# The first 1024 tokens' value projection, block by block, with TensorE run in beforehand

## The chip, the cores and the metric

The kernel runs on one core of a Trainium2 chip. What counts is the device time of one execution in microseconds (us). A core has TensorE (PE in the profile; its weight loads are PEld), VectorE (DVE), ScalarE (ACT), GpSimd (POOL) and SyncE (SP, which here issues the DMAs). PSUM, where TensorE writes its sums, has 8 banks of 128 x 512 words of 32 bits.

## The reference

A trunk of two layers over 1024 tokens of width 1024, all in float32. Layer 0 mixes tokens by dilated attention, layer 1 by gated linear attention; each mixer is followed by a squared-ReLU MLP. The change touches the very start: the first norm and the value part of the first projection.

```python
def rmsnorm(x, w):
    y = xf * lax.rsqrt(jnp.mean(xf * xf, axis=-1, keepdims=True) + NORM_EPS)
    return (y * w.astype(jnp.float32)).astype(x.dtype)

def dilated_attention(h, w_in, w_out):
    qkv = (h @ w_in).reshape(B, S, N_GROUPS, 3, ATTN_HEADS, HEAD_DIM)   # 3 groups
    ...
        v = qkv[:, :, g, 2].astype(jnp.float32)
    ...

h = rmsnorm(x, norm_mix_w[0]);  x = x + dilated_attention(h, ...)
```

So for each of three column groups g a 1024 x 1024 matrix of weights is applied to the normed tokens to give the values.

## The kernel before

A product in float32 is made of three in a rounded format: each operand is a rounded part ("hi", written by ScalarE: `dh` for weights, `a12h` for tokens) and a remainder ("lo", written by VectorE: `dl`, `a12l`), and hi x hi, hi x lo and lo x hi are summed in one bank.

The value projection uses Strassen's scheme (Winograd's form): tokens and columns are halved, and seven products of half matrices take the place of eight. The token operands are `a11`, `a12` (first 512 tokens, first and second half of the width), `a21`, `a22` (last 512 tokens) and sums of them, `s1` to `s4`; `s1` is `a21 + a22`. They are made once and serve all three groups. Work goes in *steps*, numbered n = 14 g + 2 q + m: group g, product q (0 to 6), half m of the depth. A step has 24 products of 128 x 512: 4 blocks of 128 tokens, 2 slices of depth, 3 combinations. Steps 0 and 1 multiply `a12` into the four banks `pB`, steps 2 and 3 `a11` into four banks `pA`; steps 4 and 5 (`s1`) follow in `pB`, 6 and 7 (`s2`) in `pA`, 8 and 9 (`s4`) in `pB`. Steps 14 and 15 are steps 0 and 1 of group 1: the same `a12`, other weights.

The class `Values` has a method for each part of a step: `load` (512 KB of weights, a DMA from SP), `total` (VectorE's sum of weight blocks, where the scheme has one), `rounded` (`dh`, L808), `remain` (`dl`, L814), `product` (the matmuls, L829), `sums` (`copy`, ScalarE takes a bank out, L839; `add`, VectorE adds the other bank, L844, and SP stores the result `c`). The first product's banks are copied out as `c11` when its step is done, and the second's are added. `prep` is `rounded` and `remain`.

The class `Halves` makes the token operands, in pairs of blocks (256 tokens): `norm` (ScalarE squares and sums a row, L243; VectorE and ScalarE make the root; VectorE scales, giving `xn`, L252), `turn` (TensorE transposes 128 x 128 pieces of `xn` with `ident` into a bank `pT`, L334; ScalarE copies it out into `a`, L336), `cut` (ScalarE rounds `a`, L344, VectorE takes the remainder, L346).

There is no scheduler: each engine's instructions stand in the order in which the code issues them, and each engine works its list in order, waiting where an operand or a buffer is not ready. Buffers come from pools: `h8` (12 of 8 KB for each partition), `k4` (25 of 4 KB, for weights in all forms and `xn`), `t2` (8 of 2 KB), and the 8 banks. The order at the start is written out by hand, and from step 8 on is a loop:

```python
for n in range(8, vals.STEPS):
    ...
    vals.sums(n)
    vals.prep(n + 2)
    vals.load(n + 5)
    vals.product(n)
```

At the start, steps 0 to 3 are done for blocks 0 and 1 as soon as these two blocks are turned and cut, then for blocks 2 and 3, and then step 4 follows; blocks 4 to 7 are normed and turned in between, since `s1` needs them.

Of the kernel before, what the change touches and what calls it, by code (L numbers as in the profile page):

```python
# [19 lines left out]
P = 128  # L20
D = 1024
S = 1024
NB = S // P
# [6 lines left out]
EPS = 1e-5  # L30
# [11 lines left out]
def hybrid_trunk(ctx, tc, x, norm_mix, norm_mlp, norm_fin, a_in, a_out, g_in, g_up, g_b, g_nw,  # L42
                 g_out, m_up, m_down, tab, msk, gmask, ident_d, out):
    nc = tc.nc
    pe, act, dve, pool, sp = nc.tensor, nc.scalar, nc.vector, nc.gpsimd, nc.sync
# [454 lines left out]
    class Up:  # L500
# [244 lines left out]
    class Values:  # L745

        STEPS = 14 * NG
        small = False
        BLOCKS = ((1, 0), (0, 0), (0, 1), (1, 1), (1, 1), None, (1, 0))

        def __init__(self):
# [7 lines left out]
        def load(self, n):  # L759
# [3 lines left out]
            if q == 5:  # L763
                return
            k, c = self.BLOCKS[q]
            if q in (1, 2):
# [63 lines left out]
                                  stop=m == 1 and k == 1 and v == 2, skip_group_check=True)  # L830

        def copy(self, name, s, t, g):
            if name == "c22":
                if t % 2 == 0:
                    self.pair = k4([P, 2, 512], F32, "c22")
# [15 lines left out]
        def sums(self, n):  # L851

            g, q, m = self.place(n)
            if q == 0 and g and m == 0:
                for t in range(4):
                    self.add("c21", "B", t, g - 1)
            for t in (2 * m, 2 * m + 1):
                if q == 1:
                    self.copy("c11", "B", t, g)
# [18 lines left out]
    class Mixed(Values):  # L878

        STEPS = 28  # L880
        small = True

        def __init__(self):
            super().__init__()
# [80 lines left out]
    scale = HD ** -0.5  # L965
# [299 lines left out]
            at(t + 10, lambda half=half: join(half), 9)  # L1265


    x0 = []
    vals = Values()
    for p in range(NB // 2):  # L1270
        t = h8([P, 2, D], F32, "x0")
        for i in range(2):
            sp.dma_start(t[:, i, :], x[0, 256 * p + 128 * i:256 * p + 128 * i + 128, :])
        x0.append(t)
        if p == 0:
            wbc = load_norm_w(norm_mix[0])
            sp.dma_start(ident, ident_d)
            for n in range(4):
                vals.load(n)
# [5 lines left out]
    vals.remain(0)  # L1285
    hs.cut("a12", 0)
    hs.turn(0, (0, 1))
    vals.prep(1)
    hs.cut("a11", 0)
    vals.prep(2)  # L1290
    vals.prep(3)
    hs.norm(1)
    for n in range(3):
        vals.product(n, [0, 1])
    hs.norm(2)
    hs.turn(1)
    vals.product(3, [0, 1])
    hs.cut("a12", 1)
    hs.cut("a11", 1)
    vals.load(4)  # L1300
    vals.load(5)
    hs.turn(2)
    hs.sum1(0)
    vals.total(4)
    hs.rstd(3)
    hs.norm(3)
    for n in range(2):
        vals.product(n, [2, 3])
    hs.cut("s1", 0)
    vals.rounded(4)  # L1310
    hs.turn(3)
    vals.remain(4)
    vals.product(2, [2, 3])
    vals.total(5)
    vals.sums(2)
    hs.sum1(1)
    hs.cut("s1", 1)
    vals.sums(3)
    vals.rounded(5)
    vals.product(3, [2, 3])  # L1320
    vals.remain(5)
    vals.load(6)
    vals.load(7)
# [3 lines left out]
    hs.cut("s2", 0)  # L1327
    vals.rounded(6)
    hs.cut("s2", 1)
    vals.sums(4)  # L1330
    vals.sums(5)
    vals.remain(6)
    vals.load(8)
    vals.product(4)
# [2 lines left out]
    vals.product(5)  # L1337
    for c in range(2):
        hs.cut("s4", c)
    hs.sum3()  # L1340
    vals.load(9)
    for n in range(6, 8):
        vals.sums(n)
        vals.load(n + 4)
        vals.product(n)
        vals.prep(n + 2)
        if n == 6:
            for c in range(2):
                hs.cut("s3", c)
        else:  # L1350
            for c in range(2):
                hs.cut("a22", c)
    vals.load(12)
    for n in range(8, vals.STEPS):
        if n == 12:
            ctab = h8([P, 2, S], F32, "tab")
            sp.dma_start(ctab[:, 0, :], tab[:, 0, :])
            sp.dma_start(ctab[0:64, 1, :], tab[64:128, 1, :])
            sp.dma_start(ctab[64:128, 1, :], tab[0:64, 1, :])
        if n == vals.STEPS - 2:  # L1360
            heads = Heads(vals.h)
# [7 lines left out]
        vals.prep(n + 2)  # L1369
        vals.load(n + 5)  # L1370
        vals.product(n)
    for t in range(4):
        vals.add("c21", "B", t, NG - 1)
# [630 lines left out]
    for half in range(2):  # L2004
        ps = bank("pd")
# [7 lines left out]
        l = lrT[:, 512 * half:512 * half + 512]  # L2013
# [62 lines left out]
```

## Time and profile before

| | |
|---|---|
| median of 3 runs | 2612.7 us (2612.32 to 2613.21) |
| the profiled execution | 2613.06 us, span 2611.3 us |
| mean granted TensorE clock | 0.999 |
| first instruction of TensorE | 8.89 us |
| first product of the value projection | 12.96 us |
| first product of step 4 | 44.58 us |

The span goes from the first to the last instruction; times of single instructions are counted from its start. A row of the timeline gives start, length, engine, line, operation, what it writes and reads, how many follow each other, and in brackets for how long the engine stood idle before and for whom it waited. Matmuls are pipelined: a row's length (0.39 us) is longer than the distance to the next start.

### The profile page before, as it was taken

What the parts mean: (1) busy time and instruction counts of PE and PEld (TensorE: products, weight loads), DVE (VectorE), ACT (ScalarE), POOL (GpSimd) and SP (SyncE); (2) the same over time, 40 slices, a digit from 0 to 9 for tenths busy, and PEclk for the clock granted to TensorE, in tenths of its full rate; (3) what the DMA queues carried; (4) which work ended last, traced back from release to release, by engine and by line L of the source; (5) the groups of instructions that cost most, each with busy time, mean ns of one, the idle gap of its engine ahead of it and who ended that gap; (6) DMA issues with size and microseconds to landing.
All of it is one profiled execution on the core that took longest, in us unless ns stands there. A gap on an engine that the chain in (4) does not pass through costs nothing.

```text
span 2611.3 us, 33042 instructions
## 1 busy us (share of the span) xinstructions
PE 2586.3 (99%) x12144; PEld 2157.3 (83%) x12144; DVE 1858.9 (71%) x2986; ACT 1276.7 (49%) x2319; POOL 1.8 (0%) x7
## 2 busy tenths in 40 slices
PE   8999999999999999999999999999999999999998
PEld 6888888888888888888888887878888888888887
DVE  7645888888888768666657577977658866666566
ACT  6332455555556446555533345654326545553343
POOL 0000000000000000000000000000000000000000
PEclk9999999999999999999999999999999999999999
DMA  5533465655556733454775452463513544396543
GB/s 190 169 129 124 103 161 131 163 147 150 155 151 183 227 121 128 167 169 137 283 252 185 137 194 93 133 199 97 187 66 123 170 153 157 131 355 200 189 146 125
DMA packets 327010, 423.12 MB, mean 162 GB/s; under 512 B 19808, under 2 KB 192224, under 8 KB 326848
## 3 DMA queue, kind: packets, MB, share of 16 engines
q1 hardware_dynamic: 326848, 421.01, 51.0%
q8 instruction: 95, 1.56, 0.3%
q14 instruction: 67, 0.55, 0.1%
HBM read 279.71 MB, written 116.06 MB: 152 GB/s over the span
## 4 chain that ended last, share of the span: by engine, by line
PE 87%; DVE 8%; ACT 3%; issue 1%; DMA 1%; SPq 0%; ACTq 0%; DVEq 0%
PE pX L598 16%; PE pB L1581 13%; PE pV L598 11%; PE pA L1581 10%; PE pY L598 5%; PE pZ L598 5%; PE pB L829 5%; PE pd L215 3%; PE pd L213 3%; PE pd L214 3%; PE pA L829 3%; PE pO L1017 2%; PE pS L976 2%; PE pP L1003 1%; DVE dl L814 1%
## 5 line engine op out<-in xcount | busy, mean ns | idle before, releaser
L1581 PE MATMUL pB<-dh 128*128 128x512 f32 x512 | 199.4, 389 | 0.0
L1581 PE MATMUL pB<-dh,dl 128*128 128x512 f32 x512 | 199.2, 389 | 0.0
L1581 PE MATMUL pB<-dl,dh 128*128 128x512 f32 x512 | 199.2, 389 | 0.0
L222 DVE TENSOR_TENSOR dl<-sin,dh 128x1024 fp32r<-128x1024 f32 x112 | 136.5, 1218 | 44.6 <-ACT dh L219 44.2
L219 ACT ACTIVATE dh<-sin 128x1024 fp32r<-128x1024 f32 x112 | 117.8, 1052 | 89.7 <-PE pB L1581 32.5
L219 ACT ACTIVATE dh<-kept 128x1024 fp32r<-128x1024 f32 x64 | 67.9, 1061 | 183.4 <-DVE kept L1546 137.8
L598 PE MATMUL pV<-s4h,wd 128*128 128x512 f32 x448 | 150.8, 398 | 0.0
L1581 PE MATMUL pA<-dh,dl 128*128 128x512 f32 x384 | 149.4, 389 | 0.0
L1581 PE MATMUL pA<-dl,dh 128*128 128x512 f32 x384 | 149.4, 389 | 0.0
L1581 PE MATMUL pA<-dh 128*128 128x512 f32 x384 | 149.4, 389 | 0.0
L992 ACT ACTIVATE pt<-pt,orow 128x128 f32<-128x128 f32 (+1 forms) x192 | 84.8, 443 | 96.7 <-DVE orow L990 94.6
L1581 PEld LDWEIGHTS pB<-dh,dl 128*128 128x128 f32 x512 | 96.1, 188 | 20.1
L1581 PEld LDWEIGHTS pB<-dh 128*128 128x128 f32 x512 | 96.1, 188 | 19.9
L1581 PEld LDWEIGHTS pB<-dl,dh 128*128 128x128 f32 x512 | 96.1, 188 | 19.8
L536 DVE TENSOR_TENSOR wal<-raw,wah 128x512 fp32r<-128x512 f32 x112 | 76.2, 686 | 42.9 <-ACT wah L535 42.9
L607 ACT ACTIVATE c<-c 128x512 f32<-128x512 f32 x64 | 40.4, 632 | 122.6 <-DVE c L635 78.9
L598 PEld LDWEIGHTS pV<-s4h,wd 128*128 128x128 f32 x448 | 84.2, 188 | 17.7 <-DVE rb L623 0.2
L222 DVE TENSOR_TENSOR dl<-kept,dh 128x1024 fp32r<-128x1024 f32 x64 | 78.3, 1224 | 25.1 <-ACT dh L219 19.3
L536 DVE TENSOR_TENSOR wbl<-t,wbh 128x1024 fp32r<-128x1024 f32 x56 | 68.6, 1225 | 38.3 <-ACT wbh L535 38.3
L990 DVE CUSTOM_DVE_ANT_0 pt<-pS,masks 128x128 f32<-128x128 f32 (+1 forms) x192 | 58.2, 347 | 51.2 <-PE pS L976 51.2
L598 PE MATMUL pY<-a12h,wah 128*128 128x512 f32 x224 | 89.5, 400 | 0.0
L598 PE MATMUL pZ<-a22h,wgh 128*128 128x512 f32 x224 | 89.3, 399 | 0.0
(336 smaller groups left out, 7364.2 us busy)
## 6 DMA issues: line engine op xcount, KB each, us to landing
sin<-acts SPq DMA_DIRECT2D x112, 512.0 KB, 3.8
raw<-in_mlp_w_up_dram SPq DMA_DIRECT2D x64, 512.0 KB, 6.0
acts<-s SPq DMA_DIRECT2D x64, 512.0 KB, 3.4
raw<-in_mlp_w_down_dram SPq DMA_DIRECT2D x64, 512.0 KB, 4.7
raw<-in_attn_w_in_dram SPq DMA_DIRECT2D x96, 256.0 KB, 4.6
cw<-c SPq DMA_DIRECT2D x192, 128.0 KB, 2.3
acts<-c SPq DMA_DIRECT2D x64, 256.0 KB, 2.1
kept<-in_mlp_w_down_dram SPq DMA_DIRECT2D x32, 512.0 KB, 5.8
```

The costliest lines, as they stand in the source:

```text
L213: pe.matmul(ps, sh, mh, start=start, stop=False)
L214: pe.matmul(ps, sh, ml, start=False, stop=False)
L215: pe.matmul(ps, sl, mh, start=False, stop=stop)
L219: act.activation(hi, src, AF.Copy)
L222: dve.tensor_tensor(lo, src, hi.bitcast(F32), op=OP.subtract)
L536: self.remain(lambda: dve.tensor_tensor(lo, src, hi.bitcast(F32), op=OP.subtract))
L598: pe.matmul(st[b], u[:, k, :], v, start=first and k + n == 0, stop=k == 3 and n == 2, skip_group_check=True)
L829: pe.matmul(self.acc[s][t], a[:, c], b[:, k, :], start=fresh and m + k + v == 0, stop=m == 1 and k == 1 and v == 2, skip_group_check=True)
L976: pe.matmul(ps[:, i, :128 * n], self.qT[:, 128 * b:128 * b + 128], self.kT[:, k0:k0 + 128 * n], start=True, stop=True)
L990: dve.tensor_tensor_reduce(pt[:, i, :128 * n], ps[:, i, :128 * n], masks[:, m0:m0 + 128 * n], -scale, 1e38, op0=OP.add, op1=OP.min, accum_ ...
L992: act.activation(pt[:, i, :128 * n], pt[:, i, :128 * n], AF.Exp, scale=-1.0, bias=m, accum_out=self.row[:, r, HD:HD + 1])
L1581: pe.matmul(self.acc[s][t], a[:, k, c], b[:, k, :], start=fresh and m + k + v == 0, stop=m == 7 and k == 1 and v == 2, skip_group_check=True)
```

## The change

It rewrites the order of the start and has these parts.

- Run-in: POOL clears a tile `warm`, and TensorE does 26 matmuls of 128 x 512 in bf16 on it, before anything else.
- Loads: the first block's rows and the norm weight `wbc` come in halves; the order on SP becomes first block, half of `wbc`, `ident`, weights of step 0, other half of `wbc`, weights of step 1, block 1, weights of steps 2 and 3, blocks 2 to 5, weights of steps 14 and 15, blocks 6 and 7.
- Blocks 0 to 3 are handled singly: `sq` and `lne` make the root's start on ScalarE, `nvz` one Newton step on VectorE, `xn` half a block, `tr` four transposes into one bank. `hi` and `lo` round and take the remainder straight from that bank; `ac` copies it into `a` later (the sums need it).
- Products: steps 0 to 3 are done for block 0 first, then block 1, 2 and 3; after blocks 4 and 5 are turned, steps 14 and 15 on block 0, then blocks 6 and 7 are turned, then steps 14 and 15 on blocks 1 to 3, then step 4.
- The `c11` of group 1 is copied out then, into two buffers of `k4`, and kept until the add of step 18. The later loop leaves out steps 14 and 15 (`plan`); the adds of group 0's last product (`c21`) move from step 14 to step 16.
- `sums(2)` to `sums(5)` stand earlier (`cp`, `ad`); after step 6, `cut("s3")` and `sum3` stand one later.

```diff
-    x0 = []
+    x0 = [h8([P, 2, D], F32, "x0") for _ in range(NB // 2)]
...
+    warm = t2([P, 512], BF16, "warm")
+    pool.memset(warm, 0.0)
+    dve.memset(eps, EPS)
+    ps = bank("warm")
+    for _ in range(26):
+        pe.matmul(ps, warm[:, 0:P], warm, start=True, stop=True)
+    for c in (0, 512):
+        sp.dma_start(x0[0][:, 0, c:c + 512], x[0, 0:128, c:c + 512])
...
+    load_wbc(512)
+    sp.dma_start(ident, ident_d)
+    vals.load(0)
+    load_wbc(0)
+    vals.load(1)
+    load_rows(1)
+    vals.load(2)
+    vals.load(3)
+    load_rows(2, 3, 4, 5)
+    vals.load(14)
+    vals.load(15)
+    load_rows(6, 7)
...
+    def sq(b):
+        r = root0[b] = sm([P, 8], "root")
+        junk = t2([P, D], BF16, "junk")
+        act.activation(junk, rows0(b), AF.Square, accum_out=r[:, 0:1])
+    def lne(b):
+        r = root0[b]
+        act.activation(r[:, 2:3], r[:, 0:1], AF.Ln, scale=1.0 / D, bias=eps)
+        act.activation(r[:, 3:4], r[:, 2:3], AF.Exp, scale=-0.5)
+    def nvz(b):
+        ss, nv, t, y, z = (root0[b][:, i:i + 1] for i in range(5))
+        dve.tensor_scalar(nv, ss, -0.5 / D, -0.5 * EPS, op0=OP.mult, op1=OP.add)
+        dve.scalar_tensor_tensor(z, y, nv, y, op0=OP.mult, op1=OP.mult)
+        dve.scalar_tensor_tensor(z, z, 1.5, y, op0=OP.add, op1=OP.mult)
...
+    def hi(b, half):
+        ps, h, l, a = spot(b, half)
+        act.activation(h, ps, AF.Copy)
+    def lo(b, half):
+        ps, h, l, a = spot(b, half)
+        dve.tensor_tensor(l, ps, h.bitcast(F32), op=OP.subtract)
+    def ac(b, half):
+        ps, h, l, a = spot(b, half)
+        act.activation(a, ps, AF.Copy)
...
-    hs.norm(0, (512, 768, 0, 256), 256)
-    vals.rounded(0)
-    hs.turn(0, (2, 3))
...
-    for n in range(3):
-        vals.product(n, [0, 1])
-    hs.norm(2)
-    hs.turn(1)
-    vals.product(3, [0, 1])
...
+    hi(0, 1)
+    lo(0, 1)
+    xn(0, 0)
+    rh(1)
+    pr(0, 0)
+    sq(1)
+    rl(1)
+    tr(0, 0)
+    lne(1)
+    hi(0, 0)
+    rh(2)
+    nvz(1)
+    xn(1, 1)
+    pr(1, 0)
...
+    rh(15)
+    pr(1, 3)
+    ad(1)
+    rl(15)
+    hs.xn[2] = [xn0.pop(4), xn0.pop(5)]
+    pr(2, 3)
+    hs.turn(2)
+    sq(7)
...
+    pr(14, 0)
+    hs.xn[3] = [xn0.pop(6), xn0.pop(7)]
+    pr(15, 0)
+    hs.turn(3)
+    hs.cut("s1", 0)
     vals.load(4)
     vals.load(5)
...
-    for n in range(8, vals.STEPS):
+    plan = [n for n in range(8, vals.STEPS) if n // 14 not in vals.ahead or n % 14 > 1]
...
+        if n % 14 == 2 and n // 14 in vals.ahead:
+            for t in range(4):
+                vals.add("c21", "B", t, n // 14 - 1)
```

(`rh`, `rl`, `pr` are `rounded`, `remain` and `product` on the named blocks; `cp`, `ad` are `copy` and `add` of `c11`.)

How the order stands, first on TensorE at its beginning. The numbers behind the names tell one tile from another: `pB_213` and `pB_214` are the banks of blocks 0 and 1, `dh_142`/`dl_158` the weights of step 0. Before, behind sixteen transposes:

```order
L334 MATMUL pT_170<-ident_68,xn_133 128x128
L829 MATMUL pB_213<-dh_142,a12h_160 128x512
L829 MATMUL pB_213<-dl_158,a12h_160 128x512
L829 MATMUL pB_213<-dh_142,a12l_161 128x512
L829 MATMUL pB_214<-dh_142,a12h_160 128x512
L829 MATMUL pB_214<-dl_158,a12h_160 128x512
L829 MATMUL pB_214<-dh_142,a12l_161 128x512
```

Now, behind the run-in (`pB_187` is block 0's bank, `dh_173` of step 0, `dh_185` of step 1, `dh_210` of step 2; `xn_171` is block 0, `xn_215` block 1):

```order
L1342 MATMUL pT_175<-ident_68,xn_171 128x128 x4
L830 MATMUL pB_187<-dh_173,a12h_154 128x512
L830 MATMUL pB_187<-dl_180,a12h_154 128x512
L830 MATMUL pB_187<-dh_173,a12l_155 128x512
...
L1342 MATMUL pT_202<-ident_68,xn_171 128x128 x4
L830 MATMUL pB_187<-dh_185,a12h_154 128x512
...
L1342 MATMUL pT_226<-ident_68,xn_215 128x128 x4
L830 MATMUL pA_235<-dh_210,a11h_156 128x512
```

Six products of one block now stand behind four transposes, and step 1 behind four more.

VectorE at the same place, before:

```order
L252 SCALAR_TENSOR_TENSOR xn_133<-x0_93,y_123,wbc_96 128x256
L814 TENSOR_TENSOR dl_158<-raw_99,dh_142 128x1024
L346 TENSOR_TENSOR a12l_161<-a_145,a12h_160 128x4x256
L814 TENSOR_TENSOR dl_178<-raw_101,dh_176 128x1024
L346 TENSOR_TENSOR a11l_181<-a_144,a11h_180 128x4x256
L814 TENSOR_TENSOR dl_186<-kept_103,dh_184 128x1024
```

and now:

```order
L815 TENSOR_TENSOR dl_200<-raw_136,dh_185 128x1024
L1328 TENSOR_SCALAR root_197<-root_197 128x1
L1329 SCALAR_TENSOR_TENSOR root_197<-root_197 128x1
L1330 SCALAR_TENSOR_TENSOR root_197<-root_197 128x1
L1336 SCALAR_TENSOR_TENSOR xn_215<-x0_93,root_197,wbc_130 128x512
L1354 TENSOR_TENSOR a11l_157<-pT_202,a11h_156 128x4x128
L815 TENSOR_TENSOR dl_224<-kept_139,dh_210 128x1024
L1336 SCALAR_TENSOR_TENSOR xn_215<-x0_93,root_197,wbc_130 128x512
L815 TENSOR_TENSOR dl_245<-kept_141,dh_232 128x1024
L1354 TENSOR_TENSOR a12l_155<-pT_226,a12h_154 128x4x128
```

Block 1's root and `xn` now stand between the weights' remainders of steps 1, 2 and 3, and remainders of tokens are taken from a bank.

TensorE once more, where the last blocks are turned. Before, the transposes of blocks 6 and 7 (`xn_370`, `xn_371`) stood between steps 1 and 2 of blocks 2 and 3:

```order
L829 MATMUL pB_216<-dh_176,a12l_161 128x512
L334 MATMUL pT_408<-ident_68,xn_370 128x128
L334 MATMUL pT_408<-ident_68,xn_371 128x128
...
L334 MATMUL pT_426<-ident_68,xn_371 128x128
L829 MATMUL pA_243<-dh_184,a11h_180 128x512
```

Now step 3 of block 3 (`pA_238`) and steps 14 and 15 of block 0 (`dh_410`, `dh_418`) stand ahead of them (`xn_407`), behind the last bank of blocks 4 and 5 (`xn_396`):

```order
L334 MATMUL pT_456<-ident_68,xn_396 128x128
L830 MATMUL pA_238<-dh_232,a11h_156 128x512
L830 MATMUL pA_238<-dl_245,a11h_156 128x512
...
L830 MATMUL pB_489<-dh_410,a12h_154 128x512
L830 MATMUL pB_489<-dl_412,a12h_154 128x512
...
L830 MATMUL pB_489<-dh_418,a12h_154 128x512
...
L334 MATMUL pT_505<-ident_68,xn_407 128x128
```

Products of group 1 thus stand between the turns of blocks 4, 5 and of blocks 6, 7.

More of the change, by code (lines that the diff above doesn't have):

```diff
@@ L748, in hybrid_trunk @@
         small = False
+        ahead = (1,)
         BLOCKS = ((1, 0), (0, 0), (0, 1), (1, 1), (1, 1), None, (1, 0))
@@ L832, in copy @@
         def copy(self, name, s, t, g):
-            if name == "c22":
+            if name == "c22" or (name == "c11" and g in self.ahead):
                 if t % 2 == 0:
-                    self.pair = k4([P, 2, 512], F32, "c22")
+                    self.pair = k4([P, 2, 512], F32, name)
                 c = self.pair[:, t % 2, :]
@@ L858, in sums @@
                 if q == 1:
-                    self.copy("c11", "B", t, g)
+                    if g not in self.ahead:
+                        self.copy("c11", "B", t, g)
                 elif q == 2:
@@ L881, in hybrid_trunk @@
         small = True
+        ahead = ()
         def __init__(self):
@@ L1265, in plan_merges @@
             at(t + 10, lambda half=half: join(half), 9)
-    x0 = []
+    x0 = [h8([P, 2, D], F32, "x0") for _ in range(NB // 2)]
     vals = Values()
[L1270 to L1279, printed above, removed]
+    eps = sm([P, 1], "eps")
@@ new lines, in rows0, with load_rows @@
+    def rows0(b):
+        return x0[b // 2][:, b % 2, :]
+    def load_rows(*bs):
+        for b in bs:
+            sp.dma_start(rows0(b), x[0, 128 * b:128 * b + 128, :])
+    warm = t2([P, 512], BF16, "warm")
[6 more added lines that the diff above has]
+        sp.dma_start(x0[0][:, 0, c:c + 512], x[0, 0:128, c:c + 512])
+    wbc, row = k4([P, D], F32, "wbc"), norm_mix[0]
@@ L1280, in hybrid_trunk, with load_wbc @@
+    def load_wbc(c):
+        sp.dma_start(wbc[:, c:c + 512], bass.AP(tensor=row.tensor, offset=row.offset + c, ap=[[0, P], [1, 512]]))
+    load_wbc(512)
[10 more added lines that the diff above has]
+    load_rows(6, 7)
     sp.dma_start(masks, msk)
     hs = Halves(x0, wbc, vals, None)
-    hs.norm(0, (512, 768, 0, 256), 256)
-    vals.rounded(0)
@@ L1284, in hybrid_trunk @@
-    hs.turn(0, (2, 3))
[L1285 to L1292, printed above, removed]
-    for n in range(3):
-        vals.product(n, [0, 1])
-    hs.norm(2)
-    hs.turn(1)
-    vals.product(3, [0, 1])
-    hs.cut("a12", 1)
-    hs.cut("a11", 1)
+    for name in ("a12", "a11"):
+        vals.h[name] = Split(hs.one(name + "h", F32R), hs.one(name + "l", F32R))
+    for half in range(2):
+        hs.a[0, half] = hs.one("a", F32)
@@ new lines, in xn, with tr, spot @@
+    def xn(b, half):
+        if b not in xn0:
+            xn0[b] = k4([P, D], F32, "xn")
+        sl = slice(512 * half, 512 * half + 512)
+        dve.scalar_tensor_tensor(xn0[b][:, sl], rows0(b)[:, sl], root0[b][:, 4:5], wbc[:, sl], op0=OP.mult, op1=OP.mult)
+    def tr(b, half):
+        ps = face[b, half] = bank("pT").rearrange("p (k t) -> p k t", k=4)
+        for k in range(4):
+            c = 512 * half + 128 * k
+            pe.transpose(ps[:, k, :], xn0[b][:, c:c + 128], ident)
+    def spot(b, half):
+        s, sl = vals.h[("a11", "a12")[half]], slice(128 * b, 128 * b + 128)
+        return face[b, half], s.hi[0][:, :, sl], s.lo[0][:, :, sl], hs.a[0, half][0][:, :, sl]
@@ new lines, in hi, with pr @@
+    def hi(b, half):
[7 more added lines that the diff above has]
+        act.activation(a, ps, AF.Copy)
+    def pr(n, *ts):
+        vals.product(n, list(ts))
+    rh, rl = vals.rounded, vals.remain
+    cp = lambda t, g=0: vals.copy("c11", "B", t, g)
+    ad = lambda t: vals.add("c11", "A", t, 0)
@@ new lines, in hybrid_trunk @@
+    r = root0[0] = sm([P, 8], "root")
+    junk = t2([P, D], BF16, "junk")
+    act.activation(junk[:, 0:512], x0[0][:, 0, 0:512], AF.Square, accum_out=r[:, 5:6])
+    act.activation(junk[:, 512:], x0[0][:, 0, 512:], AF.Square, accum_out=r[:, 6:7])
+    dve.tensor_scalar(r[:, 7:8], r[:, 5:6], 1.0 / D, EPS, op0=OP.mult, op1=OP.add)
+    act.activation(r[:, 2:3], r[:, 6:7], AF.Ln, scale=1.0 / D, bias=r[:, 7:8])
+    act.activation(r[:, 3:4], r[:, 2:3], AF.Exp, scale=-0.5)
+    dve.tensor_tensor(r[:, 0:1], r[:, 5:6], r[:, 6:7], op=OP.add)
@@ new lines, in hybrid_trunk @@
+    nvz(0)
+    xn(0, 1)
+    rh(0)
+    tr(0, 1)
+    rl(0)
+    hi(0, 1)
[12 more added lines that the diff above has]
+    pr(1, 0)
+    lo(0, 0)
+    rl(2)
+    tr(1, 1)
+    hi(1, 1)
+    rh(3)
+    xn(1, 0)
+    pr(2, 0)
+    rl(3)
+    lo(1, 1)
+    sq(2)
+    lne(2)
+    tr(1, 0)
+    pr(3, 0)
+    hi(1, 0)
+    nvz(2)
+    xn(2, 1)
+    lo(1, 0)
+    xn(2, 0)
+    ac(0, 1)
+    pr(0, 1)
@@ new lines, in hybrid_trunk @@
+    pr(1, 1)
+    ac(0, 0)
+    sq(3)
+    lne(3)
+    cp(0)
+    tr(2, 1)
+    hi(2, 1)
+    pr(2, 1)
+    nvz(3)
+    xn(3, 1)
+    lo(2, 1)
+    tr(2, 0)
+    hi(2, 0)
+    xn(3, 0)
+    lo(2, 0)
+    ac(1, 1)
+    ac(1, 0)
+    pr(3, 1)
+    pr(0, 2)
+    sq(4)
+    lne(4)
+    ad(0)
+    cp(1)
+    tr(3, 1)
+    hi(3, 1)
+    pr(1, 2)
+    nvz(4)
+    xn(4, 1)
+    lo(3, 1)
+    tr(3, 0)
+    hi(3, 0)
+    xn(4, 0)
+    lo(3, 0)
+    pr(2, 2)
+    sq(5)
+    lne(5)
+    ac(2, 1)
+    ac(2, 0)
@@ new lines, in hybrid_trunk @@
+    nvz(5)
+    pr(3, 2)
+    pr(0, 3)
+    xn(5, 1)
+    xn(5, 0)
+    sq(6)
+    lne(6)
+    nvz(6)
+    xn(6, 1)
+    xn(6, 0)
+    rh(14)
+    rl(14)
+    cp(2)
+    ac(3, 1)
+    ac(3, 0)
+    rh(15)
[6 more added lines that the diff above has]
+    sq(7)
+    lne(7)
+    pr(3, 3)
+    nvz(7)
+    xn(7, 1)
+    xn(7, 0)
+    cp(3)
+    hs.sum1(0)
+    ad(2)
+    pr(14, 0)
+    hs.xn[3] = [xn0.pop(6), xn0.pop(7)]
+    pr(15, 0)
@@ L1300, in hybrid_trunk @@
+    hs.turn(3)
+    hs.cut("s1", 0)
     vals.load(4)
     vals.load(5)
-    hs.turn(2)
-    hs.sum1(0)
-    vals.total(4)
[L1305 to L1309, printed above, removed]
+    cp(0, 1)
+    pr(14, 1)
+    pr(15, 1)
+    ad(3)
+    hs.sum1(1)
+    cp(1, 1)
+    vals.total(4)
+    hs.cut("s1", 1)
     vals.rounded(4)
-    hs.turn(3)
+    pr(14, 2)
+    pr(15, 2)
     vals.remain(4)
-    vals.product(2, [2, 3])
+    cp(2, 1)
     vals.total(5)
-    vals.sums(2)
@@ L1316, in hybrid_trunk @@
-    hs.sum1(1)
-    hs.cut("s1", 1)
-    vals.sums(3)
+    pr(14, 3)
+    pr(15, 3)
+    cp(3, 1)
     vals.rounded(5)
-    vals.product(3, [2, 3])
     vals.remain(5)
@@ L1343, in hybrid_trunk @@
         vals.sums(n)
+        if n == 7:
+            for c in range(2):
+                hs.cut("s3", c)
         vals.load(n + 4)
@@ L1347, in hybrid_trunk @@
         if n == 6:
-            for c in range(2):
-                hs.cut("s3", c)
+            hs.sum3()
         else:
@@ L1353, in hybrid_trunk @@
     vals.load(12)
-    for n in range(8, vals.STEPS):
+    plan = [n for n in range(8, vals.STEPS) if n // 14 not in vals.ahead or n % 14 > 1]
+    plan += range(vals.STEPS, vals.STEPS + 5)
+    for i, n in enumerate(plan[:-5]):
         if n == 12:
@@ L1367, in hybrid_trunk @@
             heads.stage(0, 3)
+        if n % 14 == 2 and n // 14 in vals.ahead:
+            for t in range(4):
+                vals.add("c21", "B", t, n // 14 - 1)
         vals.sums(n)
-        vals.prep(n + 2)
-        vals.load(n + 5)
+        vals.prep(plan[i + 2])
+        vals.load(plan[i + 5])
         vals.product(n)
```

4 lines of the change are left out of this document (1 added, 3 removed).

## The prediction

> **What bounds the kernel now.** I read the page's first part, then the waits of TensorE over the first 120 us, then five stretches of that time, and only then single instructions.
>
> ```profile
> PE 2586.3 (99%) x12144; PEld 2157.3 (83%) x12144; DVE 1858.9 (71%) x2986; ACT 1276.7 (49%) x2319; POOL 1.8 (0%) x7
> ```
>
> TensorE is busy for 2586.3 of 2611.3 us. The change moves products and neither adds nor removes one of them, so it can only win TensorE's idle time back, and only where it reorders: the first 70 us. The waits there (engine, line, what ended them, total, times, longest) and the stretches (length, PE busy and count, granted clock, DMA share and GB/s):
>
> ```profile
> PE pT L334 <- DVE xn L252: 10.4, 7, 8.9
> PE pB L829 <- DVE dl L814: 0.5, 1, 0.5
> PE pB L829 <- DVE a12l L346: 0.5, 1, 0.5
> ```
>
> ```profile
> 0.00:12.94 12.94, 3.85 (x16) 1.00 0.88 305
> 12.94:19.36 6.42, 5.88 (x25) 1.00 1.03 411
> 19.36:44.58 25.22, 23.49 (x122) 1.00 0.30 104
> 44.58:70.00 25.42, 24.89 (x110) 1.00 0.44 145
> 70.00:160.00 90.00, 90.00 (x399) 1.00 0.44 146
> ```
>
> The last stretch has no gap: 90 us hold 397 to 399 starts, so a product costs 0.227 us when the next follows at once. The bounds of the others are starts of instructions:
>
> ```profile
> 8.89 3.85 PE L334 MATMUL pT<-ident,xn 128*128 128x128 f32 x16 [8.89 <-DVE xn L252]
> 9.29 3.46 PE L334 MATMUL pT<-ident,xn 128*128 128x128 f32 x15
> 12.96 0.50 PE L829 MATMUL pB<-dh,a12h 128*128 128x512 f32 x1 [0.21 <-ACT a12h L344]
> 13.30 0.39 PE L829 MATMUL pB<-dl,a12h 128*128 128x512 f32 x1
> 14.22 0.50 PE L829 MATMUL pB<-dh,a12l 128*128 128x512 f32 x1 [0.53 <-DVE a12l L346]
> 19.36 0.39 PE L829 MATMUL pA<-dh,a11h 128*128 128x512 f32 x1
> 28.04 1.91 PE L334 MATMUL pT<-ident,xn 128*128 128x128 f32 x16
> 44.58 0.39 PE L829 MATMUL pB<-dh,s1h 128*128 128x512 f32 x1
> 66.44 0.39 PE L829 MATMUL pB<-dh,s4h 128*128 128x512 f32 x1
> 67.36 0.50 PE L829 MATMUL pB<-dl,s4h 128*128 128x512 f32 x1 [0.53 <-DVE dl L814]
> ```
>
> Sixteen transposes take 1.91 us at 28.04, 0.108 each; at the start fifteen take 3.46, so TensorE then ran at half its pace, although the row of 0.00 to 12.94 says 1.00. From 13.30 it runs at the full one: the half pace lasted from 8.89 to about 12.9, 4 us.
>
> Three losses follow. (1) The 24th product ends at 19.36; 24 products and 16 transposes are 7.2 us of work, so 12.2 us are idle or at half pace. (2) From 19.36 to 44.58 stand 72 products and 48 transposes: 16.34 + 5.18 = 21.5 of 25.22 us, 3.7 lost, in the waits on `xn`. (3) At 66.44 the second product of step 8 comes 0.92 us after the first, and 0.1 more goes as it starts again: 0.8 lost. Together 16.7 us; the question is how much of it remains.
>
> **The change, part by part.** Durations come from these rows:
>
> ```profile
> 4.50 1.06 ACT L243 ACTIVATE junk<-x 128x1024 bf16<-128x1024 f32 x1 [2.49 <-DMA x<-in_x_dram]
> 9.79 1.06 ACT L808 ACTIVATE dh<-raw 128x1024 fp32r<-128x1024 f32 x1 [2.25 <-DMA raw<-in_attn_w_in_dram]
> 15.66 2.00 ACT L808 ACTIVATE dh<-kept 128x1024 fp32r<-128x1024 f32 x2
> 17.13 2.35 DVE L814 TENSOR_TENSOR dl<-kept,dh 128x1024 fp32r<-128x1024 f32 x2
> 18.51 0.19 ACT L243 ACTIVATION_READ_ACCUMULATOR junk<-x 128x1 f32 x1
> 19.97 0.20 ACT L230 ACTIVATE t<-v 128x2 f32<-128x2 f32 x1 [0.23 <-DVE v L229]
> 20.64 0.16 DVE L233 TENSOR_TENSOR t<-t,v 128x2 f32<-128x2 f32 x1
> 21.24 2.74 DVE L252 SCALAR_TENSOR_TENSOR xn<-x,y,wbc 128x512 f32<-128x512 f32 x4
> 24.44 2.04 ACT L336 ACTIVATE a<-pT 128x512 f32<-128x512 f32 x4
> 51.97 1.28 DVE L844 TENSOR_TENSOR c<-pA,c 128x512 f32<-128x512 f32 x2
> ```
>
> So: square of a block 1.05 (0.19 more for its sum), each small ACT step 0.24, each small DVE step 0.20, half a block's `xn` 0.67, a half's rounding out of a bank 0.52 on ACT, its remainder 0.62 on DVE (nearest row: the add that reads `pA`), a weight part's `dh` 0.95 to 1.06 and `dl` 1.16.
>
> *Loads.* The first row below gives 408 GB/s, 1.28 us for 512 KB. The first block has landed by 4.50; half of it is asked for alone and should land near 3.5. The first weight part lands at 9.79 as the last of 2.16 MB; now 1.38 MB end with it, 0.79 MB less, so 7.85. The second is then the last of 2.16 MB (9.8), and block 1's rows follow at 11.05.
>
> ```profile
> 10.00:20.00 10.00, 9.27 (x40) 7.35 (x39) 8.77 (x12) 9.73 (x15) 0.00 (x0) 1.00 1.04 408
> 0.73 1.28 ACT L735 ACT_TABLE_LOAD   x1 [0.73 <-PEq L2065]
> L1726 POOL MEMSET gc<- 128x512 f32 x1 | 0.5, 524 | 975.2 <-DVE wal L536 975.2
> ```
>
> *The run-in.* POOL clears its tile in 0.5 us (the last row, twice the bytes) after the engines start at 0.73 (the row above it), so the 26 products begin near 1.3. No row has a bf16 product; I take the 0.227 of the 128x512 product, doubled at half pace. Nine fill its 4 us, 17 more take 3.9: they end at 9.3. Bounds: 7.2, if there were no half pace, 13.1, if it never ended. TensorE works in order, so the first transposes wait for that, though `xn` is there at 6.9 (second half landed 4.5, square and root to 5.8, two small DVE steps, 0.67). The run-in hides the half pace but holds the chain.
>
> *Block 0 and block 1.* Transposes 9.3 to 9.95; rounded `a12h` 10.5; ACT then takes the second `dh` (10.5 to 11.45), the square of block 1 (from 11.45, its rows landed 11.05) and its root: 13.05. From there VectorE is never free: two small steps 13.45, `xn` 14.1, block 0's other remainder 14.75, `dl` of step 2 15.9, `xn` 16.55, `dl` of step 3 17.7, block 1's remainder 18.35. Products of steps 0 to 2 fit between. Step 3 on block 0 gets its `dl` at 17.7 and five products later, at **18.9**, the 24th is done: 0.45 us ahead of before. So a first product 2.5 us earlier (10.5 against 12.96) is worth 0.45, because VectorE's chain sets the pace.
>
> *From there to the end of steps 14 and 15.* 72 products, 48 transposes and the 48 products moved ahead. The moved 48 are 10.9 us of cover for VectorE, not a gain. Supplies, laid out the same way, against TensorE's need: remainder of block 2 at 23.5 (needed 25.2), of block 3 at 29.0 (31.5), `dl` of steps 14 and 15 at 36.9 and 38.3 (38.6, 40.0). Waits I find: 0.2 where `pB` of block 3 takes the bank of a transposed half that ACT copies out late (ACT is full from 11 to 38 us); 0.4 to 1.0, taken 0.7, where the fourth bank of blocks 4 and 5 waits for ACT's copy of the first, queued behind the `dh` of step 15; 0.25 to 0.5, taken 0.4, for block 7's second `xn` near 42.3. To that come twelve changes between transposes and products instead of eight, 0.4, and 0.2 for the loads of steps 4 and 5: in SP's queue they now stand behind three stores of `c`, the last of which waits for VectorE until 44, so they land near 48.6, when VectorE comes to them. Sum **1.9**, against 3.7 lost before: 1.8 gained.
>
> *After.* The copies and adds that stood before step 6 are done by then, but step 8's `dl` ends only 0.6 us before its need. I leave half of the 0.8: **0.4** gained. The two held buffers cost nothing, since each load up to step 18 takes a buffer whose last reader is done before the load's turn in SP's queue; nor do the c21 adds, moved from step 14 to step 16, where only bank reads precede the products.
>
> Sum: 0.45 + 1.8 + 0.4 = 2.6 us. The profiled execution took 2613.06 us, 2611.3 of it the span; that is 0.4 over the median of 2612.7. A span of 2608.7 puts the median at **2610.1**.
>
> [...] Before, the pace doubled after sixteen transposes alone. [...]
>
> **The rivals.**
>
> *All waits go* (16 in 100). If ACT's copies keep pace and step 8 finds its `dl`, only the 0.4 of changes remains: 0.45 + 3.3 + 0.8 = 4.6, and up to 1.3 more if block 1's rows land one transfer sooner: 2606.8 to 2608.1. For it: every wait above is under a microsecond of a 40 us chain. Against: ACT has no slack there.
>
> *The cover is there but the start is late* (15). If the half pace lasts longer, each of its microseconds holds the transposes by half of one; an end at 10.6 instead of 9.3 delays all of VectorE's chain by 1.3, and the same ACT queue doubles the 1.3 us of waits behind it. 2611.4 to 2612.7: the change does not do what it says.
>
> *Slower* (7). Between 9.3 and 18.9 TensorE works only 7.2 of 9.6 us, in pieces of 0.4 to 1.4. If its pace falls back to half there, 24 products and 16 transposes need 14.4 us, TensorE becomes the bound, and the 24th ends at 24.3: 5.4 later than laid out, 2615.5. Each such microsecond after that costs half of one more, so it passes 0.2% (5.2 us, what a measurement of this kernel tells from no change) if the half pace lasts to 29 us. Against: before kept its pace over gaps of 0.5; the longest here is 1.3. [...]
>
> **How the numbers follow.** The layout above has 62, for 2610.1. The range goes from 2607.2 to 2613.0: most of the first rival, all of the second, not the third; 12 in 100 are left out. Under 2607.5 lies half of the first rival and a rest of the layout, so faster has 0.10; slower is the third, 0.07; the rest, 0.83, is within 0.2%.
>
> **What would show it.** The run-in ending near 9.3 and the first `pB` near 10.5; the 24th product near 18.9, behind a `dl`; VectorE without a gap from 13 to 38; a wait of under 1 us at the fourth bank of blocks 4 and 5 and one for block 7's `xn`; the first `s1h` product at 52 to 53.5 (44.58 + 10.9 - 2.2 = 53.3); from 85 us on, nothing. I am wrong if the 24th product ends outside 18 to 20, if steps 14 and 15 wait for their `dl`, or if the time from step 8 on differs.

## The result, and the profile after

| | before | after |
|---|---|---|
| time, median of 4 runs each | 2612.93 us | 2648.02 us |
| range | 2612.32 to 2613.21 | 2647.72 to 2648.11 |
| span of the profiled execution | 2611.3 us | 2646.2 us |

The ratio after to before is 1.0134, with a 95% interval of 1.0122 to 1.0146. The forecast was 2610.1, from 2607.2 to 2613.0: the kernel became 35.1 us slower, and no case of the forecast reached so far.

The first part of the page says which engine has the time:

```profile
PE 2629.6 (99%) x12170; PEld 2160.9 (82%) x12170; DVE 1864.6 (70%) x2993; ACT 1280.2 (48%) x2333; POOL 2.3 (0%) x8
```

TensorE is busy 43.3 us longer (2586.3 before). The 26 run-in products, which fill 1.31 to 8.8, explain some 7.6 of it. The other 35.7 are not waiting time: TensorE's waits over the whole span come to 7.5 us, these above all (total, times, longest):

```profile
PE pA L830 <- DVE dl L815: 1.6, 2, 0.8
PE pB L830 <- ACT a12h L1350: 1.4, 1, 1.4
PE warm L1287 <- POOL warm L1283: 1.3, 1, 1.3
PE pB L830 <- DVE c L845: 1.3, 1, 1.3
PE pB L830 <- DVE dl L815: 1.0, 2, 0.8
PE pd L215 <- DVE oTl L222: 0.7, 1, 0.7
```

So the same products take longer. Three stretches with next to no gap, far behind the change, show where (length, PE busy and count of starts, granted clock, DMA share and GB/s). Before:

```profile
70.00:160.00 90.00, 90.00 (x399) 1.00 0.44 146
1000.00:1290.00 290.00, 289.94 (x1278) 1.00 0.51 171
1310.00:1550.00 240.00, 240.00 (x1060) 1.00 0.57 191
```

After:

```profile
70.00:160.00 90.00, 90.00 (x387) 1.00 0.46 146
1000.00:1290.00 290.00, 290.00 (x1246) 1.00 0.45 150
1310.00:1550.00 240.00, 240.00 (x1061) 1.00 0.61 209
```

In the value steps (the first stretch) and in the MLP's first half, Up (the second), fewer products start in the same time; in its second half, Down (the third), as many as before. The granted clock reads 1.00 in all six rows. From start to start a product takes 226.7 to 226.8 ns before in all three stretches, and 233.3, 233.1 and 226.7 after. The change from one pitch to the other falls between two neighbouring instructions (the timeline of after, TensorE):

```profile
2015.21 0.39 PE L215 MATMUL pd<-whi,o1l 128*128 128x512 f32 x1
...
2017.48 0.40 PE L598 MATMUL pX<-a11h,wah 128*128 128x512 f32 x1
...
2019.81 0.40 PE L598 MATMUL pX<-a11l,wah 128*128 128x512 f32 x1
```

From the first of these rows to the second there are ten products in 2.27 us, from the second to the third ten in 2.33. Both are 128x512, both run back to back. What differs is their operands: `whi` and `o1l` both lie in the k4 pool, `a11h` in h8 and `wah` in k4.

**Where the operands lie.** The change creates `eps` (of the pool sm) and `warm` (of t2) before the first k4 tile, and in the built program the pools follow each other in SBUF in the order in which each had its first tile. Before, h8 (12 buffers of 8192 bytes, from 3200) was followed by k4, at 101504. Now sm (19 of 96 bytes) and t2 (8 of 2080) stand between them, and k4 begins at 119968. The difference between k4 and h8 was 98304 bytes, 0 after division by 256; now it is 116768, which leaves 32. Value steps and Up multiply an h8 operand by a k4 operand, Down two k4 operands. I matched the trace's products with the program's operands. The sum is best read against c_place (below), which has the same instructions in the same order at the old addresses. Counted are the products that the next one follows without a pause; the columns give the mean time to the next start, in ns, and what all of them together take longer in after, in us:

| operands | products | c_place | after | longer by |
|---|---|---|---|---|
| moving from h8, stationary from k4 (as in Up) | 4205 | 227.4 | 233.2 | 24.3 |
| moving from k4, stationary from h8 (as in the value steps) | 1544 | 227.5 | 233.4 | 9.2 |
| both from k4, the next product's mixed | 821 | 227.1 | 231.9 | 4.0 |
| both from k4, the next product's too | 3331 | 226.8 | 226.8 | 0.0 |

That is 37.5 us. All else, waits above all, is 1.8 us shorter in after, which leaves the 35.7 between the spans of the two (2646.2 and 2610.5).

**The first 56 us.** What the prediction was about shows here (the rows of TensorE):

```profile
0.00:9.40 9.40, 8.09 (x30) 1.00 0.72 206
8.54:11.95 3.41, 1.70 (x8) 1.00 1.03 381
11.95:15.37 3.42, 3.35 (x11) 0.50 1.05 408
15.37:21.63 6.26, 5.32 (x26) 1.00 1.04 402
```

The run-in gives its place to the transposes at 8.80, the first product starts at 10.84, and then the granted clock falls to half for 3.42 us. The loads are late too. On ACT, the second weight part and block 1's rows:

```profile
9.24 1.06 ACT L809 ACTIVATE dh<-raw 128x1024 fp32r<-128x1024 f32 x1 [3.34 <-DMA raw<-in_attn_w_in_dram]
...
12.47 1.06 ACT L809 ACTIVATE dh<-raw 128x1024 fp32r<-128x1024 f32 x1 [1.68 <-DMA raw<-in_attn_w_in_dram]
13.79 1.06 ACT L1319 ACTIVATE junk<-x 128x1024 bf16<-128x1024 f32 x1 [0.26 <-DMA x<-in_x_dram]
```

The layout had the first weight part (the first row) at 7.85, these two at 9.8 and 11.05. The 24th product ends at 21.6, where the layout had 18.9 and before 19.36.

### The profile page after: what moved, and what is told of

Read it like the earlier page. It is cut to its first block, busy times and chain, and to the rows that moved or that the text cites. A ratio compares the mean times of both kernels' runs of the same rounds, so it can differ in the third digit from the quotient of the medians.

```text
span 2646.2 us, 33128 instructions
## 1 busy us (share of the span) xinstructions
PE 2629.6 (99%) x12170; PEld 2160.9 (82%) x12170; DVE 1864.6 (70%) x2993; ACT 1280.2 (48%) x2333; POOL 2.3 (0%) x8
## 4 chain that ended last, share of the span: by engine, by line
PE 96%; DVE 2%; ACT 1%; DMA 1%; issue 0%; SPq 0%; ACTq 0%; DVEq 0%
PE pX L598 18%; PE pB L1771 13%; PE pV L598 12%; PE pA L1771 10%; PE pB L830 7%; PE pZ L598 6%; PE pY L598 6%; PE pA L830 4%; PE pd L215 3%; PE pd L213 3%; PE pd L214 3%; PE pO L1020 2%; PE pS L979 2%; PE pP L1006 1%; PE pT L334 1%; PE pO L2027 1%
## 5 line engine op out<-in xcount | busy, mean ns | idle before, releaser
L219 ACT ACTIVATE dh<-sin 128x1024 fp32r<-128x1024 f32 x112 | 118.0, 1053 | 89.1 <-PE pB L1771 32.4
L1771 PEld LDWEIGHTS pB<-dh,dl 128*128 128x128 f32 x512 | 96.1, 188 | 19.9
L603 ACT ACTIVATE e<-pX 128x512 f32<-128x512 f32 x96 | 56.5, 589 | 80.9 <-PE pX L598 80.9
```

The source lines that it names most:

```text
L219: act.activation(hi, src, AF.Copy)
L1771: pe.matmul(self.acc[s][t], a[:, k, c], b[:, k, :], start=fresh and m + k + v == 0, stop=m == 7 and k == 1 and v == 2, skip_group_check=True)
```

## The experiments

**Is it the addresses?** Theory A says that the pitch depends on where the two operands lie; theory B, that the bf16 run-in or the new order puts TensorE into a slower pace that lasts. Four kernels move the pools and do next to nothing else. The first two give the small tiles more buffers:

```diff
-        return wk.tile(shape, F32, name=name, tag="sm", bufs=19)
+        return wk.tile(shape, F32, name=name, tag="sm", bufs=20)   # a_sm20; 22 in a_sm22
```

> The changed kernel with one edit: the pool of small tiles holds 20 buffers instead of 19. No instruction and no order changes, only the SBUF address at which the k4 tiles (weights) begin: 120064 bytes instead of 119968, which is 0 instead of 32 after division by 64; the h8 tiles (tokens) lie at 0 in both. Theory A (placement): a 128x512 product takes 233 ns where its moving operand and the stationary operand loaded under it lie differently within 64 bytes, 227 where they lie alike. Then 5,600 products get 6.4 ns back, about 36 us, and the time is 2611 to 2613. Theory B (the run-in's bf16 products, or the new order, put TensorE into a slower pace that lasts): nothing changes, 2648, pitch 233.

> As the run before, with 22 small buffers: k4 then begins at 64 after division by 128, but at 0 after division by 64. Theory A with a 64-byte period: 2611 to 2613. Theory A with a 128-byte period: 2648, as after the change. Theory B: 2648 too, but then the run with 20 buffers stays there as well.

The other two start from the kernel before, without run-in or new order. They make two tiles that nothing reads, either behind the first h8 tile (b_k4shift) or ahead of it (b_allshift):

```diff
+    first = h8([P, 2, D], F32, "x0")
+    pad_s, pad_t = sm([P, 1], "pad_s"), t2([P, 512], BF16, "pad_t")
+    dve.memset(pad_s, EPS)
+    pool.memset(pad_t, 0.0)
...
```

> The kernel before, with two tiles that nothing reads (one small, one of the t2 pool), made and cleared after the first h8 tile and before the first k4 tile. That puts k4 at 32 after division by 64 and leaves h8 at 0, as the change does; run-in and order are those of before. Theory A: 2647 to 2650, pitch 233 in the value and Up stages, 227 in the Down stages. Theory B: 2613, pitch 227 throughout.

> The kernel before with the same two unread tiles made ahead of the first h8 tile, so that h8 and k4 both begin at 32 after division by 64. If only the difference between the two operands counts (theory A, relative): 2613, pitch 227. If each operand must lie at 0 itself (theory A, absolute): 2648 or more, since then the Down stages have the longer pitch too. Theory B: 2613.

The kernel before with two unread tiles and nothing else takes 2647.25 (ratio 1.0129, 1.0114 to 1.0145), 33.7 us over the runs of before beside it (2613.52): all but some 1.4 of the 35.1, without one instruction of the change on TensorE. With both pools shifted alike it takes 2613.66 (1.0000, 0.9991 to 1.0010). So theory B has fallen, and it is the difference between the pools that counts, not where either lies. The stretch 1000 to 1290 of b_k4shift, and then of b_allshift:

```profile
1000.00:1290.00 290.00, 290.00 (x1246) 1.00 0.45 149
```

```profile
1000.00:1290.00 290.00, 289.96 (x1279) 1.00 0.50 170
```

My period of 64 bytes was wrong, though: with 20 buffers the time is 2637.9 (1.0094, 1.0079 to 1.0109) and with 22 it is 2643.85 (1.0117, 1.0101 to 1.0134), where I had 2611 to 2613 for both. Their differences leave 128 and 64 after division by 256. The pitch of products with mixed operands is 231.8 (moving from h8) and 232.5 (moving from k4) in a_sm20, 232.9 and 229.4 in a_sm22. So I looked for a longer period, with two placements of the full change.

**The change without the shift.** In c_place the tile `wbc`, the first of k4, is made ahead of `eps` and `warm`, which puts k4 back to 101504; in a_p256 it is made between `warm` and `eps`, which leaves a difference of 256 within 512.

```diff
+    wbc, row = k4([P, D], F32, "wbc"), norm_mix[0]
     eps = sm([P, 1], "eps")
     ...
     for c in (0, 512):
         sp.dma_start(x0[0][:, 0, c:c + 512], x[0, 0:128, c:c + 512])
-    wbc, row = k4([P, D], F32, "wbc"), norm_mix[0]
```

> The changed kernel, in which the tile wbc (the first of the k4 pool) is made one line earlier, ahead of the first small tile and the first t2 tile. No instruction and no order changes; k4 then begins at 101504 as before the change, 98304 bytes = 192 x 512 after h8. After the first four runs the theory of placement reads: full pace (227 ns) only where the two operands lie alike within 512 bytes; the runs with 20 and 22 small buffers left 128 and 320 bytes, and their products took 229 to 235. Theory A, so refined: pitch 227 throughout, and the rest of the change is worth 0.4 to 1.3 us: 2611.6 to 2613.1 on a before of 2613.0 to 2613.5. Theory C (20 buffers left 25 us unexplained because the change itself, run-in or order, costs them): 2636 to 2638.

> The changed kernel with wbc made after the first t2 tile and before the first small one: the 8 x 2080 bytes of t2 alone then lie between h8 and k4, a difference of 256 within 512. Period 512: 2630 to 2648. Period 256 or less (with 128 excluded by the run with 20 buffers, whose difference is 128): 2611 to 2613.

c_place takes 2614.14 (1.0004, 0.9995 to 1.0013) and a_p256 2613.81 (1.0003, 0.9994 to 1.0012): one line, moved, gives 33.9 us back, and theory C falls. A difference of 256 is as good as 0, while 32, 64 and 128 are not, so among these sizes the period, if there is one, is 256 bytes. The eight placements together (pitches in ns, means over all products of the stretch that follow each other without a pause):

| kernel | k4 minus h8, after division by 256 | pitch 70 to 160 us | 1000 to 1290 | 1310 to 1550 | time, us |
|---|---|---|---|---|---|
| before | 0 | 226.7 | 226.8 | 226.7 | 2612.9 |
| b_allshift | 0 | 226.7 | 226.7 | 226.7 | 2613.7 |
| a_p256 | 0 | 226.7 | 226.7 | 226.7 | 2613.8 |
| c_place | 0 | 226.7 | 226.8 | 226.7 | 2614.1 |
| after | 32 | 233.3 | 233.1 | 226.7 | 2648.0 |
| b_k4shift | 32 | 233.3 | 233.1 | 226.7 | 2647.3 |
| a_sm22 | 64 | 228.9 | 233.1 | 226.7 | 2643.9 |
| a_sm20 | 128 | 233.0 | 231.3 | 226.7 | 2637.9 |

The last stretch, with both operands in k4, is the control: it is the same in all eight. Why a difference costs 2 to 7 ns, and why in a_sm22 one direction costs so much less than the other, these runs do not show.

**What the rest of the change is worth.** With the placement restored, the start can be read by itself. The median of c_place is 1.2 us over that of the runs of before beside it (2612.98), no difference that can be measured; but its runs spread from 2612.6 to 2614.9, wider than those of before (2612.3 to 2613.9). Three kernels look for the reason, all with `wbc` made first: no run-in (`range(1)` for `range(26)`, c_norun), the norm weights in one load (c_wbc), and both (d_nrwbc).

```diff
-    load_wbc(512)
+    sp.dma_start(wbc, bass.AP(tensor=row.tensor, offset=row.offset, ap=[[0, P], [1, D]]))
...
-    load_wbc(0)
```

> The kernel of the first run of this group with 1 run-in product instead of 26. The half pace at the start then lasts to about 12.9 as before the change, but not from 11.95 to 15.37 as after it. If the loads of block 1 (13.8 us) set the start, the time is that of the first run of this group within 0.5. If the run-in is worth what it was laid out for, 1 to 2 us more.

> The kernel of the first run of this group, with the norm weights loaded by one transfer as before the change instead of two halves. In the changed kernel the second weight part landed at 12.45 and block 1 at 13.77, where the layout had 9.8 and 11.05; the second half of wbc stood between them. If the two halves cost what two whole transfers do, block 1 lands 1.3 to 2.6 us sooner, the 24th product ends 1 to 2 us sooner, and the time is 0.5 to 2 us under the first run of this group. If the queue is only limited by bytes, nothing changes (within 0.3).

> The kernel with wbc made first and 1 run-in product (2612.0), with the norm weights in one load. With the run-in this cost 0.8, but its profile had two stretches of half pace. Without the run-in, if the transfer as such matters: a shift of the loads of block 1 by 0.5 to 2.6 us shows as 0.3 to 1 us in the time. If not: 2612.0 within 0.3.

c_norun takes 2611.97 (0.9996, 0.9987 to 1.0005), 2.2 less than with the run-in; c_wbc 2614.91 (1.0008, 1.0000 to 1.0017) and d_nrwbc 2613.18 (0.9999, 0.9990 to 1.0008). By the medians the run-in costs time, against both expectations, and one load is worse than two, by 0.8 and 1.2 us (0.8 and 0.9 when each is taken against the runs of before beside it). The intervals of these four overlap. In the profiles block 1 has landed by 12.64 (c_wbc) and at 12.59 (d_nrwbc) with one load; with two it lands anywhere from 12.08 (c_place) over 13.12 (c_norun) to 13.79 (after), although these three issue the same loads in the same order. So one profile of each does not tell whether the split makes the loads late, and c_place's is an early one: none of its eleven runs has a span under this one's 2610.5 (the median is 2612.0).

The profiles do not show why the run-in should cost time either. In them it puts c_place ahead: its 24th product ends at 19.9 and c_norun's at 22.1, and of these 2.2 us 1.4 are left at 1685 us and 0.4 at the end. But c_norun's profiled span, 2610.9, lies above its median of 2610.2. Over all runs c_norun stays the faster, by 1.8 us of the median span; the reason is open.

Even in c_place the loads are late against the layout, and the stretch from 3 to 7 us is slow. The rate (last column, GB/s) there, where the layout reckoned with 408:

```profile
3.00:4.00 1.00, 1.00 (x4) 1.00 0.87 180
4.00:5.00 1.00, 1.00 (x5) 1.00 0.83 135
5.00:6.00 1.00, 1.00 (x6) 1.00 0.86 173
6.00:7.00 1.00, 1.00 (x7) 1.00 0.85 269
```

In these 4 us before moves 373, 406, 274 and 198 GB/s, 0.49 MB more, and is slow from 5 to 7 us alone, while the same transfers, `wbc` and `ident`, are under way. The DMA engines are busy 0.83 to 0.87 of this time; which of the two transfers is the slow one I did not separate.

**The granted clock.** In c_place's profile the clock stays full from 4.86 on, to the end of the products; in those of after, a_sm20 and c_wbc it falls to half for 3.4 to 6.8 us at the start (in c_wbc once more at 1738.6, for 3.4). c_wbc, and then c_place:

```profile
8.04:11.45 3.41, 1.33 (x8) 1.00 1.04 412
11.45:18.28 6.83, 6.67 (x17) 0.50 1.04 405
```

```profile
8.27:11.69 3.42, 2.00 (x9) 1.00 1.05 411
11.69:15.10 3.41, 3.24 (x15) 1.00 1.06 402
```

The record changes in steps of 3.41 us. Where TensorE was busy for 1.33 us (c_wbc) or 1.70 (after) of such a step, the next is at half pace; where it was busy for 2.00, it is not. The busy time alone does not decide, though: steps with 1.53 us (d_noahead, from 40.53) and 1.61 (d_fill, from 1731.93) were followed by the full clock, one with 1.59 (c_wbc, from 1735.19) by half of it. To fill the gap, d_fill adds products on the cleared tile to c_place:

```diff
     tr(0, 1)
+    fill(4)        # 4 products on warm; fill(3) behind pr(0, 0) and behind pr(1, 0)
     rl(0)
```

> The changed kernel with wbc made first (pitch 227), and ten more products on the cleared tile: 4 behind the first half's transposes, 3 behind step 0's first products, 3 behind step 1's. Theory F: TensorE's pace falls back to half (12 to 15.4 us in the profile of the changed kernel, in two stretches between 12 and 20 with the norm weights in one load) because it has too little work after the run-in; with the gaps filled it stays full, and the times gather near the low end of the kernel without them, 2612.3 to 2613.0, instead of 2612.6 to 2614.9. Theory G: the half pace does not depend on how little there is to do; the same spread, median 2614.1, or 0.5 more for the fillers.

Its profile shows no half pace behind the run-in, but neither does c_place's. Over all runs the clock fits theory F: the mean granted clock reads under 0.999 in two of d_fill's eleven runs and in six of c_place's. But the times are 2613.8 to 2616.2, with a median of 2615.04 (1.0007, 0.9998 to 1.0016): not near the low end that it gave, and no better than without the fillers. Its profiled span is 2.8 us over that of c_place. Of this, 1.45 are there by the 700th product: the loads landed later (block 1 at 13.16 against 12.08). Another 0.8 come at 1733 us, in layer 1's first projection, where a product needs a bank that VectorE's add frees. Here is TensorE in before, in c_place and in d_fill:

```profile
1733.98 0.50 PE L829 MATMUL pB<-dh,a22h 128*128 128x512 f32 x1 [1.18 <-DVE c L844]
```

```profile
1733.39 0.50 PE L830 MATMUL pB<-dh,a22h 128*128 128x512 f32 x1 [1.84 <-DVE c L845]
```

```profile
1736.20 0.50 PE L830 MATMUL pB<-dh,a22h 128*128 128x512 f32 x1 [2.66 <-DVE c L845]
```

VectorE's add stands behind the cut of a weight part, for whose load ACT waited 4.4, 4.7 and 6.1 us. c_place reaches the 700th product 1.65 us sooner than before (180.76 against 182.41) and waits 0.7 longer here: a gain at the start is partly given back 1500 us later.

**What the products moved ahead are worth.** From c_norun, d_noahead puts steps 14 and 15 back to their old place, and d_early45 also loads the parts of steps 4 and 5 where those of 14 and 15 were loaded.

```diff
-        ahead = (1,)
+        ahead = ()
...
-    vals.load(14)          # d_noahead: gone; d_early45: load(4) and load(5) stand here
-    vals.load(15)
...                         # and rh, rl, pr of 14 and 15, cp(t, 1): gone
```

> The kernel with wbc made first and 1 run-in product (2612.0), but with steps 14 and 15 back at their old place: not loaded, cut or multiplied ahead. If the 48 products moved ahead are what covers VectorE's chain (the 1.8 us term of the prediction), the waits for xn and dl come back between 20 and 55 us and the time is 1 to 2 us more, 2613 to 2614. If the single blocks and the rounding from banks do it alone, it stays at 2612.0 within 0.4.

> Steps 14 and 15 at their old place as in the run before that took 2624.1, but the two weight parts of steps 4 and 5 are loaded where those of 14 and 15 were, right behind the rows of block 5, instead of behind three stores. In that run TensorE waited 7.1 us for step 4's dh, whose load had been asked for at 47.0 and 47.5 and landed near 51, and 2.8 us for the xn of block 7. Theory L (most of its 12.1 us is the late load): 7 to 9 us come back, 2615 to 2617, and the 2.8 for xn stay, with the cut of step 4 that VectorE and ACT then do without cover. Rival (VectorE's chain alone needs the cover of the 48 products): 2621 to 2624.

d_noahead takes 2624.14 (1.0042, 1.0029 to 1.0055), 12.2 us more than c_norun where I had 1 to 2, and d_early45 2624.44 (1.0044, 1.0031 to 1.0058). My reading of the first run, a late load, fell with the second: nothing came back. The waits of d_early45 (8 to 130 us), and its clock:

```profile
PE pB L830 <- ACT dh L809: 6.6, 1, 6.6
...
PE pT L334 <- DVE xn L1336: 2.8, 1, 2.8
```

```profile
45.09:58.75 13.66, 6.63 (x22) 0.50 0.56 191
```

Step 4's `dh` waits for a difference that VectorE makes behind the last `xn`, two adds of `c` and the sums and remainders of `s1`; within that chain VectorE itself waits 2.4 us for ACT's `s1h`. In the new order the chain needs the 48 products (10.9 us) as cover; without them TensorE idles, and its clock then falls to half for 13.7 us. How much of the 12 us is idling and how much half pace these two runs do not separate.

## Why the prediction was wrong

- **"The change ... can only win TensorE's idle time back, and only where it reorders", and "from 85 us on, nothing": wrong, and this is nearly the whole miss.** I took a change that adds no products to the steps to leave each product's duration alone. Two tiles created earlier moved the k4 pool by 18464 bytes, and some 6,600 products, from the first step to the last layer, took 5 to 6 ns longer each. The missing term is 37.5 us, of which shorter waits gave 1.8 back; there was none for it among the unknown costs, so the range could not hold the time.
- **The rival *Slower* had the right side and the wrong mechanism.** TensorE's pace did fall to half between 9.3 and 18.9, for 3.4 us (11.95 to 15.37 in after). That can cost 1.7 us at most, not 35. I had held the length of single gaps against it, 0.5 in before and 1.3 in the layout; in after the longest is 1.43, and a step of 3.41 us with 1.70 us of work in it was followed by half pace.
- **The run-in** was sized well (9.3; it ended at 8.8). In c_norun the half pace lasts to 16.7 us, and in its profile the 24th product ends 2.2 us later than in c_place's, so "the run-in hides the half pace" was right. But that gain does not reach the time: by the medians c_norun is 2.2 us faster, for a reason that the runs leave open.
- **Loads.** 7.85, 9.8 and 11.05 became 8.78, 10.78 and 12.08 in c_place. The 408 GB/s came from a later stretch; from 3 to 7 us the rate is 135 to 269. And the layout had no spread: the same loads brought block 1 at 12.08 in one execution and at 13.79 in another.
- **The 24th product** (18.9) ends at 19.9 in c_place, 1.0 late as its loads are, and at 21.6 in after, where block 1 lands another 1.7 later and the half pace comes on top. The 0.45 gained is 0.55 lost at best.
- **To the end of steps 14 and 15.** c_place takes 33.87 us for 120 products and 48 transposes, 32.4 of work: 1.5 lost against 1.9 laid out. The first `s1h` product is at 53.78, laid out at 53.3. Against before that is 2.2 us gained, where 1.8 were laid out, so the term held. Its reason was only partly right: d_noahead shows that the new order depends on the 48 products, but for 12 us and not for 1.8.
- **Step 8** gained all of its 0.8, not half, but 0.7 went in steps 4 to 7, most of it behind a wait for step 4's `dl` that the layout did not have: 0.1 instead of 0.4.
- **Sum.** With the placement restored and without half pace, in c_place's profile, 1.65 us are gained by the 700th product where 2.6 were laid out, and 0.7 of them go at 1733 us. Of the cases forecast, that is the start that comes late. But this profile is one of c_place's fastest executions: its median, 2614.1, lies above the forecast's range too, so even at the old addresses no gain is shown. c_norun, the best version here, is 1.0 us under before by the medians, which its interval does not tell from no change.

## What to carry to other kernels

Before judging a change that creates, renames or moves tiles, compare the address of every pool in the two built programs: here the same matmuls cost up to 3% more (233.3 ns against 226.7) when stationary and moving operand stopped lying alike within 256 bytes, with the granted clock at 1.00 and no wait to be seen. When products far from the edit are all slower by the same few ns, look at what their operands have in common. And judge a change at the start by the whole time and by several executions: in one profile each the run-in put the 24th product 2.2 us ahead, and by the medians the kernel without it is the faster one.

## What the runs showed of the hardware

- Back-to-back 128x512 fp32r products take 226.7 to 226.8 ns from start to start in the three stretches where the pools of their operands lie a multiple of 256 bytes apart (98304 and 114944 were tried), and 229 to 233 on the mean where the distance leaves 32, 64 or 128. Placement alone turned 2613.7 us (b_allshift) into 2647.3 (b_k4shift). For what reason, these runs do not show.
- The clock fell to half although TensorE paused no longer than 1.5 us (after, 9.4 to 10.84): 1.70 us of work in a step of 3.41 did not hold it, 2.00 in c_place did. Since 1.61 in d_fill held it as well, what decides stays open.
- In five of c_place's eleven runs, 2.1 to 3.6 us of the time lie outside of the span, against 1.8 in all 33 of before. This stays open.
